# Moving two steps of a block inversion ahead in the program order of a hybrid attention and DeltaNet layer, with fewer and wider transfers for its bias and queries

## The chip, the cores and the metric

One core of a Trainium2 chip runs the kernel. The metric is the device time in microseconds (us) of one execution. The kernel before took 1246.18 us in the median of three runs (1244.01 to 1246.87). One more execution was profiled; its rows are the ones that the text reads. Times inside the program are given in us from the start of the profiled span.

The engines have short names in the rows: PE multiplies matrices (PEld is its weight load), DVE, ACT and POOL work on elements, SP only issues transfers. A transfer can also be issued by ACT or POOL.

## The reference: what is computed

One layer of an encoder on 1024 tokens of width 1024, in float32. The input is normalised and projected once; the columns of the projection feed two mixers, and their outputs are concatenated, projected, added to the input, and followed by a feed-forward part:

```
xn = rmsnorm(h); proj = xn @ w_in
attn = windowed_gqa(q_a, k_a, v_a, bias, in_window, sink)   # 8 heads of 64, 2 key/value heads, window 128
gdn  = gdn_mixer(qkv_g, z_g, a_g, b_g, ...)                 # 4 heads of 128, forwards and backwards in time
h = h + concat[attn, gdn] @ w_out
h = h + square(relu(rmsnorm(h) @ w_ffn_in)) @ w_ffn_out
out = rmsnorm(h)
```

The attention works on blocks of 128 queries, each against the key block before it, its own and the next one, with a bias that depends only on the distance of key and query. The DeltaNet part works on chunks. For each chunk and head it needs the inverse of a unit triangular matrix:

```
a_mat = where(strict, beta * kk * decay, 0)
t_mat = triangular_solve(eye + a_mat, eye, lower=True)
```

and then runs over the chunks one after the other, carrying a state. The kernel takes chunks of 128 tokens, so that there are 8 chunks, 4 heads and 2 directions: 64 triangular matrices of 128 x 128.

## The kernel before, in words

A program order is written down by Python generators, and a scheduler then fills the queue of each engine. Each engine works its queue strictly in order. The function `weave` (L55) merges several generators: each yields a price for what it has just emitted, and the stream with the smallest sum of prices divided by its weight goes next. The scheduler takes the order of emission as a priority: in its own timeline it gives an engine the earliest emitted instruction that is ready, so that the queues differ from the order of emission where something is not ready. Buffers come from pools with a fixed number of slots for each tag (`pg` 24, `pt` 12, `dbl` 2, `sc`, `wr` 4, `wh` and `wl` 3; psA and psB are 4 banks of PSUM each), and an instruction that writes into a new buffer waits for the release of the old one in that slot.

**The projection stage** (L1304). One stream holds the projections of v, z and of the attention's keys, values and queries: 24-matmul blocks of 128 output columns against half of the tokens (L125 to L129, three matmuls for each product since every operand is split into a coarse and a fine part). `proj_attn` (L468) ends the stream: one pair of blocks for keys and values, then four blocks for each of the two key/value heads' queries. For each query block DVE scales the result (L500), ACT rounds it (L501), POOL makes the remainder (L502), and four transfers on SP put the two parts of the two heads into the DRAM buffer `qad` (L506), 64 partitions each.

The other stream makes the triangular matrices (`prep`, L630), inverts their 32 x 32 diagonal blocks on DVE (`eliminate`, L665), lays the inverted blocks out in both orientations (`diag_blocks`, L685, four tiles that take all `sc` slots), and then `invert` (L695) builds the inverses of the 128 x 128 matrices. `invert` has four steps, each for two chunks, both directions and all heads. A step loads the matrices (L712), takes two result tiles and clears them on POOL (L716), copies the diagonal blocks into them with eight copies of 32 partitions on ACT (L720), and then goes through four rounds of small matmuls (L726; L736 with L740; L759; L767), each followed by an eviction (L729 on ACT; L745 and L752 on DVE; L761 on ACT; L770 on DVE). ACT also copies blocks into a helper tile (L750). In the stage only steps 0 and 1 are emitted; the projections use 16 of the `pg` slots for the transposed input (8 for each half of the tokens), 5 for keys and values.

**The next stage** (L1306 to L1324) begins with `bias_table` (L527): four `pg` tiles, each loaded by four transfers of 32 partitions on SP out of the DRAM buffer `biasd`, which `bias_rows` (L513) wrote much earlier. Then one stream holds the attention (`attention`, L603), the output projection of the attention (`out_attn`), that of the DeltaNet (`out_all`) and the transposes of the next part; the other holds steps 2 and 3 of `invert`, the forward scan, and the backward scan (`scan`, L774). The attention has 16 steps (8 query blocks, 2 key/value heads). A step computes scores on PE (L550, L551), adds the bias and takes the maximum on DVE (L552), takes the exponential on ACT (L564), scales on DVE and POOL (L569), transposes on PE (L579), copies on ACT (L581) and multiplies with the values (L591). Its query tile is loaded two steps ahead by one transfer of 128 partitions that POOL issues (`query`, L597, L600). The first query of each key/value head is asked for inside `proj_attn` (L509). The result of a query block goes out on SP (L595). A scan step loads its chunk on SP (L786, L798, L800) into `sc`, `pg` and `pt` slots, and its products are all at L805.

After these come the feed-forward products, with PE occupied nearly all the time.

Of the kernel before, what the change touches and what calls it, by code (L numbers as in the profile page):

```python
# [16 lines left out]
P = 128  # L17
SEQ = 1024
# [59 lines left out]
class Block:  # L78
# [389 lines left out]
    def proj_attn(self):  # L468
# [27 lines left out]
        for kv in range(2):  # L496
            raws = self.load_w(self.w_cols(w, C_AQ + 256 * kv, 256))
            for i, half, ps in self.pair(raws):
# [4 lines left out]
                for part, t in enumerate((qh.bitcast(F32), q)):  # L503
                    o = 64 * (kv ^ part)
                    for g in range(2):
                        nc.sync.dma_start(out=self.qad[kv, 2 * i + g, o:o + 64, half * HALF:(half + 1) * HALF],  # L506
                                          in_=t[64 * g:64 * g + 64, :])
# [5 lines left out]
    def bias_rows(self):  # L513
# [11 lines left out]
        nc.sync.dma_start(out=self.biasd, in_=row.unsqueeze(1).to_broadcast([8, 32, 512]))  # L525

    def bias_table(self):  # L527
        self.bias = []
        for b in range(4):
            t = self.pg((P, 2, 3 * P))  # L530
            for m in range(4):
                src = bass.AP(tensor=self.biasd.tensor,
                              offset=self.biasd.offset + 2 * b * 32 * 512 + P - 1 - 32 * m,
                              ap=[[511, 32], [32 * 512, 2], [1, 3 * P]])
                self.nc.sync.dma_start(out=t[32 * m:32 * m + 32], in_=src)
            self.bias.append(t)
# [60 lines left out]
    def query(self, n, kv):  # L597

        q = self.pt((P, 4, P), F32R)
        self.nc.gpsimd.dma_start(out=q, in_=self.qad[kv, :, :, n * P:(n + 1) * P].rearrange("g c t -> c g t").bitcast(F32R))  # L600
        return q
# [93 lines left out]
    def invert(self, tt, steps):  # L695
# [10 lines left out]
        for i in steps:  # L706
# [11 lines left out]
            for d in range(2):  # L718
                for q in range(4):
                    nc.scalar.copy(out=t[d][blk(q), :, blk(q)], in_=ctt[d][blk(q), :, ns].rearrange("p x n -> p n x"))  # L720
# [8 lines left out]
            nc.scalar.copy(out=x32, in_=px)  # L729
            yield 1.4  # L730
            pyt, py = self.ps("psB", (P, 8, 32)), self.ps("psB", (P, 8, 32))
# [22 lines left out]
            yield 2.4  # L754
            px = self.ps("psB", (P, 8, 64))
# [493 lines left out]
    def build(self):  # L1249
        tc, nc = self.tc, self.nc  # L1250
        with (
# [8 lines left out]
            self.biasd = d("biasd", (8, 32, 512))[:]  # L1260
# [3 lines left out]
            self.qad = d("qad", (2, 4, P, SEQ))[:]  # L1264
# [5 lines left out]
    def phases(self):  # L1270
# [11 lines left out]
        for half in range(2):  # L1282
# [5 lines left out]
            else:  # L1288
# [16 lines left out]
                  (chain(self.prep(), self.eliminate(), self.diag_blocks(), self.invert(tt, (0, 1))), 100.0)))  # L1305
# [5 lines left out]
        def output():  # L1311
# [4 lines left out]
            while len(self.summed) < 4:  # L1316
# [6 lines left out]
                  (chain(self.invert(tt, (2, 3)), self.scan(0, tt[0], w_attn), self.load_wout(0, (2,)),  # L1323
# [69 lines left out]
```

## Time and profile before

| what | value |
|---|---|
| median of three runs | 1246.18 us |
| time of the profiled execution | 1245.29 us |
| its span, first to last instruction | 1243.6 us |
| mean granted TensorE clock | 0.983 |
| busy share of PE, DVE, ACT, POOL | 95%, 69%, 50%, 46% |
| moved by DMA | 187.62 MB, 151 GB/s over the span |
| SP's DMA queue, share of 16 engines | 37.2% |
| POOL's DMA queue, share of 16 engines | 2.0% |

A row of a table by stretches gives the stretch from start to end and its length, then for PE, PEld, DVE, ACT and POOL the busy time and the count, then the granted PE clock (1.00 is full), the busy share of the DMA engines and GB/s. A row of the timeline gives start, length, engine (SPq is SP's queue), line, operation, what is written and read, the count, and in brackets how long the engine had been idle and what ended that. A row of the waits says which engine waited at which line for whom: total, times, longest. A row of groups gives busy time and the mean of one in ns. PE's busy time counts modelled ends of matmuls, so 95% is not 95% of its peak.

### The profile page before, as it was taken

Reading aid. Unit: us, or ns where it says so; the run is one execution under the profiler, and the core shown is the slowest. Engines: PE = TensorE matmul, PEld = TensorE weight load, DVE = VectorE, ACT = ScalarE, POOL = GpSimd, SP = SyncE. Lnnn points to the kernel's source line nnn. Section 1 sums busy time; section 2 is a strip of 40 time slices with the busy share of each in tenths; the row PEclk is TensorE's granted clock in tenths of the full one; section 3 lists DMA queues with packets and bytes.
Section 4 is the critical chain, followed back from the end, with each engine's and each line's share of the span. In section 5 each row is a group of like instructions: output and inputs, shape, how many; then the busy total and the mean of one; then the engine's idle time right before and its main releaser. Section 6 shows DMA issues by size and latency. Waiting matters only on the chain. (4 is left out here: it accounts for less than half of the span.)

```text
span 1243.6 us, 18468 instructions
## 1 busy us (share of the span) xinstructions
PE 1179.3 (95%) x6482; PEld 962.8 (77%) x6482; DVE 854.0 (69%) x1466; ACT 620.9 (50%) x1347; POOL 574.4 (46%) x486
## 2 busy tenths in 40 slices
PE   6999999899879999997899999999999999999997
PEld 5788877778657778876788888888777888888885
DVE  4677667973378996677654453544579797887976
ACT  6455688354575752125464544545555433444343
POOL 5354312224422334234474535445365655665595
PEclk9999999899889999998999999999999999999999
DMA  6134344524746667222234444344679624434323
GB/s 240 52 117 141 104 167 140 180 81 135 172 145 172 168 220 263 96 83 84 86 120 154 151 153 144 144 158 147 214 263 320 235 84 155 152 133 138 98 89 136
DMA packets 121629, 187.62 MB, mean 151 GB/s; under 512 B 11043, under 2 KB 64416, under 8 KB 121537
## 3 DMA queue, kind: packets, MB, share of 16 engines
q1 hardware_dynamic: 96708, 152.58, 37.2%
q10 hardware_dynamic: 16381, 29.67, 6.2%
q0 software_dynamic: 8448, 4.20, 2.0%
q8 instruction: 51, 0.84, 0.3%
q14 instruction: 41, 0.34, 0.1%
HBM read 122.39 MB, written 63.49 MB: 149 GB/s over the span
## 5 line engine op out<-in xcount | busy, mean ns | idle before, releaser
L127 PE MATMUL psA<-pg,wh 128*128 128x512 f32 x416 | 164.8, 397 | 1.7 <-ACT pt L464 1.7
L129 PE MATMUL psA<-pg,wl 128*128 128x512 f32 x416 | 164.1, 395 | 0.0
L128 PE MATMUL psA<-pg,wh 128*128 128x512 f32 x416 | 163.7, 394 | 0.0
L123 POOL TENSOR_TENSOR wl<-wr,wh 128x512 fp32r<-128x512 f32 x44 | 66.7, 1536 | 159.6 <-ACT wh L122 129.4
L1168 DVE TENSOR_TENSOR pg<-pg 128x512 fp32r<-128x512 f32 x112 | 123.0, 1133 | 17.6 <-ACT pg L1167 17.6
L123 POOL TENSOR_TENSOR wh<-wr,wh 128x512 fp32r<-128x512 f32 x32 | 47.4, 1502 | 129.0 <-ACT wh L122 129.0
L128 PE MATMUL psA<-pg,pg 128*128 128x512 f32 x256 | 99.9, 392 | 0.4 <-POOL pg L123 0.3
L127 PE MATMUL psA<-pg,pg 128*128 128x512 f32 x256 | 99.3, 392 | 0.9 <-DVE pg L1213 0.9
L1085 ACT ACTIVATE pt<-pt 128x512 f32<-128x512 f32 x64 | 40.3, 632 | 119.3 <-DVE pt L1075 119.3
L129 PE MATMUL psA<-pg,pg 128*128 128x512 f32 x256 | 99.7, 390 | 0.0
L123 POOL TENSOR_TENSOR pg<-wr,pg 128x512 fp32r<-128x512 f32 x48 | 73.4, 1560 | 51.5 <-ACT pg L122 51.5
L127 PEld LDWEIGHTS psA<-pg,wh 128*128 128x128 f32 x416 | 78.6, 189 | 19.0 <-ACT pt L464 2.1
L128 PEld LDWEIGHTS psA<-pg,wh 128*128 128x128 f32 x416 | 78.6, 189 | 17.8 <-issue 0.9
L129 PEld LDWEIGHTS psA<-pg,wl 128*128 128x128 f32 x416 | 78.6, 189 | 16.8
L1167 ACT CAST pg<-pg 128x512 fp32r<-128x512 f32 x112 | 67.1, 620 | 40.4 <-DMA pg<-sd 29.3
L128 PE MATMUL psB<-pg,pg 128*128 128x512 f32 x192 | 74.9, 390 | 0.8 <-POOL pg L123 0.7
L129 PE MATMUL psB<-pg,pg 128*128 128x512 f32 x192 | 74.8, 390 | 0.2 <-DVE pg L1168 0.2
L127 PE MATMUL psB<-pg,pg 128*128 128x512 f32 x192 | 74.7, 389 | 0.0
L122 ACT CAST wh<-wr 128x512 fp32r<-128x512 f32 x76 | 43.6, 623 | 50.0 <-PE psA L128 30.0
L1075 DVE TENSOR_TENSOR pt<-psB,pt 128x512 f32<-128x512 f32 x39 | 26.9, 689 | 54.0 <-PE psB L129 29.5
L1075 DVE TENSOR_TENSOR pt<-psA,pt 128x512 f32<-128x512 f32 x39 | 26.8, 689 | 51.8 <-PE psA L129 36.3
L127 PEld LDWEIGHTS psA<-pg,pg 128*128 128x128 f32 x256 | 48.1, 188 | 12.6 <-DVE pg L1213 2.1
(395 smaller groups left out, 3265.3 us busy)
## 6 DMA issues: line engine op xcount, KB each, us to landing
sd<-pt ACTq DMA_DIRECT2D x112, 256.0 KB, 2.1
pg<-sd SPq DMA_DIRECT2D x112, 256.0 KB, 2.9
wr<-in_w_ffn_in SPq DMA_DIRECT2D x32, 512.0 KB, 3.6
wr<-in_w_in SPq DMA_DIRECT2D x22, 512.0 KB, 5.0
pg<-in_x SPq DMA_DIRECT2D x16, 512.0 KB, 6.7
wr<-in_w_ffn_out SPq DMA_DIRECT2D x16, 512.0 KB, 4.7
sc<-kvd SPq DMA_DIRECT2D x14, 512.0 KB, 6.0
kvd<-pt SPq DMA_DIRECT2D x16, 256.0 KB, 2.4
```

The source lines that it names most:

```text
L122: nc.scalar.copy(out=h, in_=raw)
L123: (eng or nc.gpsimd).tensor_tensor(out=l, in0=raw, in1=h.bitcast(F32), op=ALU.subtract)
L127: nc.tensor.matmul(ps, wh, xh, start=first, stop=False, skip_group_check=onto)
L128: nc.tensor.matmul(ps, wh, xl, start=False, stop=False, skip_group_check=onto)
L129: nc.tensor.matmul(ps, wl, xh, start=False, stop=last, skip_group_check=onto)
L1075: self.nc.vector.tensor_tensor(out=out, in0=in0, in1=in1, op=ALU.add)
L1085: self.nc.scalar.activation(out=c, in_=c, func=AF.Relu)
L1167: nc.scalar.copy(out=s[:, 0], in_=raw)
L1168: v.tensor_tensor(out=s[:, 1], in0=raw, in1=s[:, 0].bitcast(F32), op=ALU.subtract)
```

## The change

All four steps of `invert` are emitted in the projection stage, and none in the next. Inside a step, the copies of the diagonal blocks are no longer made at its beginning: those of the second direction go to DVE and are emitted behind the first round of matmuls, those of the first direction stay on ACT, are emitted behind the second round, and are tied behind the eviction L729 on ACT (`issue_after` adds that order and nothing else). The query parts are written to `qad` in another layout with one transfer of 128 partitions for each part instead of two of 64. A query tile is read by two transfers of 64 partitions on SP instead of one of 128 partitions on POOL. `biasd` holds each row 128 times instead of 32, so that each bias tile is read by one transfer of 128 partitions instead of four of 32.

```
-                    o = 64 * (kv ^ part)
-                    for g in range(2):
-                        nc.sync.dma_start(out=self.qad[kv, 2 * i + g, o:o + 64, half * HALF:(half + 1) * HALF],
-                                          in_=t[64 * g:64 * g + 64, :])
+                    nc.sync.dma_start(out=self.qad[kv, part, i, :, half * HALF:(half + 1) * HALF], in_=t)
...
-        nc.sync.dma_start(out=self.biasd, in_=row.unsqueeze(1).to_broadcast([8, 32, 512]))
+        nc.sync.dma_start(out=self.biasd, in_=row.unsqueeze(1).to_broadcast([8, P, 512]))
...
-            for m in range(4):
-                src = bass.AP(tensor=self.biasd.tensor,
-                              offset=self.biasd.offset + 2 * b * 32 * 512 + P - 1 - 32 * m,
-                              ap=[[511, 32], [32 * 512, 2], [1, 3 * P]])
-                self.nc.sync.dma_start(out=t[32 * m:32 * m + 32], in_=src)
+            src = bass.AP(tensor=self.biasd.tensor, offset=self.biasd.offset + 2 * b * P * 512 + P - 1,
+                          ap=[[511, P], [P * 512, 2], [1, 3 * P]])
+            self.nc.sync.dma_start(out=t, in_=src)
...
         q = self.pt((P, 4, P), F32R)
-        self.nc.gpsimd.dma_start(out=q, in_=self.qad[kv, :, :, n * P:(n + 1) * P].rearrange("g c t -> c g t").bitcast(F32R))
+        for part in range(2):
+            o = 64 * (kv ^ part)
+            src = self.qad[kv, part, :, :, n * P:(n + 1) * P].rearrange("i (g c) t -> c (i g) t", c=64)
+            self.nc.sync.dma_start(out=q[o:o + 64].bitcast(F32), in_=src)
...
             t = [flat(tt[d][i]) for d in range(2)]
-            for d in range(2):
+
+            def diagonal(d):
                 for q in range(4):
-                    nc.scalar.copy(out=t[d][blk(q), :, blk(q)], in_=ctt[d][blk(q), :, ns].rearrange("p x n -> p n x"))
+                    out, src = t[d][blk(q), :, blk(q)], ctt[d][blk(q), :, ns].rearrange("p x n -> p n x")
+                    nc.vector.tensor_copy(out=out, in_=src) if d else nc.scalar.copy(out=out, in_=src)
+
...
-            nc.scalar.copy(out=x32, in_=px)
+            moved = nc.scalar.copy(out=x32, in_=px)
             yield 1.4
+            diagonal(1)
...
             yield 2.4
+            with self.tc.issue_after(moved.ins):
+                diagonal(0)
...
-                  (chain(self.prep(), self.eliminate(), self.diag_blocks(), self.invert(tt, (0, 1))), 100.0)))
+                  (chain(self.prep(), self.eliminate(), self.diag_blocks(), self.invert(tt, range(4))), 100.0)))
...
-                  (chain(self.invert(tt, (2, 3)), self.scan(0, tt[0], w_attn), self.load_wout(0, (2,)),
+                  (chain(self.scan(0, tt[0], w_attn), self.load_wout(0, (2,)),
```

More of the change, by code (lines that the diff above doesn't have):

```diff
@@ L1259, in build @@
             d = lambda name, shape: dram.tile(list(shape), F32, name=name)
-            self.biasd = d("biasd", (8, 32, 512))[:]
+            self.biasd = d("biasd", (8, P, 512))[:]
             self.hd, self.sd = d("hd", (NT, P, D))[:], d("sd", (DFF // 256, 7, P, HALF))[:]
@@ L1263, in build @@
             self.zd, self.mad = d("zd", (GH, P, SEQ))[:], d("mad", (NT, P, HALF))[:]
-            self.qad = d("qad", (2, 4, P, SEQ))[:]
+            self.qad = d("qad", (2, 2, 2, P, SEQ))[:]
             self.ktd, self.qtd = d("ktd", (GH, P, SEQ))[:], d("qtd", (GH, P, SEQ))[:]
```

## The prediction

> **What bounds the kernel now.** I read the page first, for the busy shares:
>
> ```profile
> span 1243.6 us, 18468 instructions
> PE 1179.3 (95%) x6482; PEld 962.8 (77%) x6482; DVE 854.0 (69%) x1466; ACT 620.9 (50%) x1347; POOL 574.4 (46%) x486
> ```
>
> PE is the bound, and what a change can win is PE's idle time and PE's time at a lowered clock. So the second view is the table by stretches, cut where the stages meet (the columns are PE, PEld, DVE, ACT, POOL, clock, DMA):
>
> ```profile
> 260.00:299.00 39.00, 36.43 (x567) 29.33 (x566) 19.38 (x33) 26.61 (x44) 15.26 (x16) 1.00 0.34 107
> 299.00:326.00 27.00, 27.00 (x121) 22.33 (x120) 4.74 (x7) 6.82 (x11) 11.48 (x10) 1.00 0.68 180
> 326.00:369.00 43.00, 31.64 (x545) 24.25 (x543) 28.65 (x101) 32.50 (x81) 17.34 (x21) 0.80 0.57 143
> 369.00:461.00 92.00, 86.73 (x625) 70.12 (x622) 84.85 (x278) 58.48 (x168) 29.41 (x26) 1.00 0.65 188
> ...
> 526.00:535.00 9.00, 5.23 (x36) 4.09 (x34) 9.00 (x19) 2.21 (x7) 5.60 (x4) 1.00 0.35 117
> ...
> 332.00:343.00 11.00, 7.27 (x144) 5.93 (x143) 6.72 (x28) 8.23 (x24) 5.46 (x8) 0.66 0.60 142
> ```
>
> The projections end at 326; in their last 27 us PE has no gap, while DVE works 4.74 us and ACT 6.82 us. The hole is the next stretch, 326 to 369, in which the attention starts beside steps 2 and 3 of the inversion and the scan has not begun: PE idles 43.00 - 31.64 = 11.4 us, and at a mean clock of 0.80 its 31.64 busy us would be 25.3 at full clock, an estimated 6.3 us more. Together 17.7 us. From 369 to 461, attention and forward scan together, PE idles 5.3 of 92 us and DVE 7.2: both are nearly full. Which waits make the hole is told by PE's waits from 290 to 380:
>
> ```profile
> PE psB L767 <- ACT pt L761: 4.1, 3, 3.3
> PE psA L550 <- DMA pt<-qad: 2.8, 1, 2.8
> PE psA L550 <- DVE nm L552: 1.5, 1, 1.5
> PE psB L759 <- DVE pt L752: 1.4, 2, 0.8
> PE psB L805 <- DVE sc L823: 1.2, 1, 1.2
> PE psA L591 <- ACT pt L581: 1.1, 1, 1.1
> ```
>
> The longest wait at L767 (3.3) and those at L759 (1.4) belong to the inversion, 2.8 to a query that came late, 1.5 to scores that DVE had not taken off. The timelines of SP, POOL, DVE and ACT say why:
>
> ```profile
> 297.63 19.59 SPq L506 DMA_DIRECT2D qad<-pt  x20
> ...
> 332.63 0.58 SPq L535 DMA_DIRECT2D pg<-biasd  x1
> ...
> 360.17 1.24 SPq L798 DMA_DIRECT2D sc<-kvd  x1
> ...
> 306.58 1.00 POOL L600 DMA_DIRECT2D pt<-qad  x1 [5.62 <-DMA qad<-pt]
> ...
> 326.29 0.79 POOL L600 DMA_DIRECT2D pt<-qad  x1 [6.96 <-DMA qad<-pt]
> ...
> 336.93 0.42 DVE L552 CUSTOM_DVE_ANT_0 wr<-psA,pg 128x256 f32<-128x256 f32 x1 [3.96 <-DMA qad<-pt]
> ...
> 342.49 5.20 ACT L720 COPY pg<-sc 32x256 f32<-32x256 f32 x8
> ```
>
> SP's queue is full of small transfers for 20 us before the projections end, and the last bias transfer leaves only at 332.63. DVE's third score of the second attention step waits until 336.93; the row names `qad`, but that instruction reads a bias tile loaded last, so I read it as the bias. POOL stands still for 5.62 and 6.96 us because a query transfer heads its queue and `qad` isn't written yet; the query remainders (L502) behind it are what `qad` waits for. ACT spends 5.20 us in one piece on the inversion's diagonal copies, ahead of the attention's exponentials. And the scan's first load leaves at 360.17, since it needs `sc` slots that the inversion's blocks hold to the end of step 3.
>
> **The change part by part. Steps 2 and 3 move ahead of 326.** Their PE work costs what steps 0 and 1 cost among the projections, in the groups from 262 to 299 (two steps each; L736 runs side by side with L740):
>
> ```profile
> L759 PE MATMUL psB<-pt,dbl 64*64 64x64 f32 x64 | 2.9, 222 | 1.2 <-POOL pg L490 0.9 <-DVE pt L752 0.3
> ...
> L740 PE MATMUL psB<-pt,sc 32*32 32x32 f32 x64 | 2.5, 224 | 0.0
> ...
> L767 PE MATMUL psB<-pg,pt 64*64 64x64 f32 x48 | 2.3, 221 | 0.7 <-ACT pt L761 0.7
> ...
> L726 PE MATMUL psB<-sc,dbl 32*32 32x32 f32 x128 | 2.2, 227 | 0.0
> ```
>
> That is 2.9 + 2.5 + 2.3 + 2.2 = 9.9 us. PE has no gap there, so the projections end 9.9 us later, plus new stalls: between 0 (their rounds fit between blocks) and the 2.6 us that PE idled from 260 to 299 beside steps 0 and 1. I take 1.3, the middle, for the new order brings L729 ahead of the diagonal copies but the result tiles come late: by my count of slots 16 + 5 + 3 of the 24 `pg` are taken, so three of the four tiles for steps 2 and 3 wait until the first half of the transposed input is released, two blocks (48 matmuls at 27.00 / 121, 11 us) before the projections end. The first rounds (L726, L736, L759) write no result tile and need not wait; copies, L745 and L767 go into those 11 us. Queued on POOL behind the clears are L502 and weight splits; on DVE behind L745 the evictions L500, for which PE has psA banks in reserve.
>
> **The stretch after it** keeps its PE work without the inversion: 25.3 - 9.9 = 15.4 us at full clock. Gone are the waits 3.3, 1.4, 2.8 and 1.5, 9.0 of 11.4; 2.4 stay. What idle and slow clock the start of the attention then has lies between 0.9 us (15.4 at the rate of 369 to 461, 5.3 of 92) and 2.4 + 6.3 = 8.7 (the waits that stay, and all of the clock's loss). I take 5, near the middle: the scan fills PE from its first loads on, but a few us of attention alone remain. The row of 332 to 343 has the clock at 0.66 after single gaps of 2.8 and 1.5 us, so short gaps cost clock too. By the Trainium skill (TensorE: Matmul & The Clock Gate, HAM oscillation) only idle gaps over about 3.4 us lower the clock; by that the start would cost at most 2.4 and the sum would win 2.6 more. The trace disagrees with it, and decides.
>
> Sum: what stood at 369.0 stands at 326 + 9.9 + 1.3 + 15.4 + 5 = 357.6, 11.4 us earlier.
>
> **The transfers and copies.**
>
> ```profile
> L506 SPq DMA_DIRECT2D qad<-pt x32: 445/554/600, 297.6 to 333.8; - x32
> ...
> L600 POOL DMA_DIRECT2D pt<-qad x16: 740/788/1001, 306.6 to 423.0; - x16
> ...
> L535 SPq DMA_DIRECT2D pg<-biasd x16: 371/426/1352, 317.3 to 332.6; - x16
> ...
> L525 SPq DMA_DIRECT2D biasd<-pt x1: 808/808/808, 140.0 to 140.0; - x1
> ...
> L745 DVE TENSOR_SCALAR pg<-psB x12: 404/417/431, 275.1 to 363.2; 32x256 f32<-32x256 f32 x12
> ...
> L720 ACT COPY pg<-sc x24: 612/645/681, 263.7 to 347.1; 32x256 f32<-32x256 f32 x24
> ...
> pt<-qad POOLq DMA_DIRECT2D x16, 256.0 KB, 4.5
> pt<-pd SPq DMA_DIRECT2D x16, 256.0 KB, 6.7
> ```
>
> Writing `qad`: 16 issues of 0.554 go (8.9 us of SP ahead of 334). Bias: 12 issues of 0.426 go (5.1 us). These 14 us are what brings the first queries and the bias before the projections' end; their worth is in the 9.0 above, not added again. The fourfold write of `biasd` leaves at 140.0 and is first read at 317.3: 177 us cover it; at the 6.7 us in which 256 KB land below, its 2 MB would take 54, so nothing is charged, and the cover holds. Queries: 16 x 0.788 = 12.6 us leave POOL, and 32 issues come to SP, at the 0.43 to 0.55 of its neighbours 14 to 18 us over the 120 us of the attention, hidden while SP only waits; on SP's queue a load landed in 6.7 us (`pd`), on POOL's in 4.5 (`qad`). The Trainium skill says why that may be (DMA: Bandwidth & Descriptors, Queues, rings and completion order): what SP issues is consumed in ring order behind SP's own earlier loads, while an engine alternates between queues. It speaks against this move, by some 2.2 us on each query. With a lead of two attention steps I charge 0; without that cover it is the third rival. The 16 DVE copies cost between 0.417 (L745, the same shape) and 0.645 (the same copy on ACT), 6.7 to 10.3 us, of which half lies beside steps 0 and 1 and half beside 2 and 3, where DVE has 20 and 22 us free; 0, and uncovered at most 10.3 less what ACT gives up.
>
> **Later stages.** With the scan earlier against the other stream, the stretch 526 to 535, where DVE is full and PE idles 3.8 us, may close; against that the backward scan moves into the stretch where DVE is full already. Bounds +4 and -3, I take 0.
>
> In all: 1245.29 - 11.4 = 1233.9 for the profiled execution. The median of the runs is 0.9 above that execution, so 1234.8, rounded 1235. Own range of this case: best 9.9 + 0 + 15.4 + 0.9 gives 352.2 (16.8 won) and 4 more, 1225; worst 9.9 + 2.6 + 15.4 + 8.7 gives 362.6 (6.4 won) less 3, 1243.
>
> **The rivals.** *The inversion ends late.* If the clears and copies for the three late tiles don't fit into the 11 us, L767 and its waits (3.3, 1.4) stay behind the projections with half of the clock's loss (3): 11.4 - 7.7 = 3.7 won, 1242.5. For it: slots are the tightest thing here. Against: ACT and DVE are nearly empty then.
>
> *The attention can't fill PE alone.* Then the inversion was filler, and the hole reopens apart from the transfers' 2.8 and 1.5: 17.7 - 4.3 = 13.4 in place of 5, 8.4 less, 3.0 won, and with the late stages' -3 nothing: 1246. For it: ACT was busy 32.50 of 43 us, more than half with attention. Against: the scan is there at once, and from 369 on the two fill PE.
>
> *SP's queue becomes the wait, slower.* The queries now stand in one queue with the scan's loads, which wait for slots, and with the attention's stores. Waits of SP from 369 to 461, and the scores' group there:
>
> ```profile
> SPq L798 <- DVE sc L833: 7.5, 1, 7.5
> ...
> SPq L786 <- DVE wl L873: 4.0, 1, 4.0
> SPq L786 <- DMA pg<-in_w_out: 3.9, 1, 3.9
> ...
> 369.00:461.00 92.00, 19.36 (x80) 1.00 0.65 188
> ```
>
> 80 rows, 8 to a step, are 10 steps, 9.2 us each. A query's lead is 18.4 us, less 6.7 to land 11.7. It decides once SP stands longer than 11.7 us before a query: 7.5 + 4.0 + 3.9 = 15.4 in a row would make a step 3.7 us late. At half of the 10 steps that is 18.5 us against 11.4: 7.1 slower, 1253. Against: these waits lie apart, and the scheduler places the query by its own timeline.
>
> **How the numbers follow.** A measurement of this kernel can tell about 0.2% (2.5 us) from no change. The forecast has 0.62, all faster but 0.01; the late inversion 0.13 (0.09 faster, 0.04 same); the unfilled attention 0.12 (0.05 faster, 0.07 same); the SP queue 0.13, slower. Faster 0.75, same 0.12, slower 0.13. The range 1226 to 1247 takes in the first three cases nearly whole and leaves out the slower one.
>
> **What would show it.** Right: L726 to L770 of all four steps before the projections' end, which comes near 337; no wait of L550 for `qad` or of L552 for a transfer; the first scan load before 345; clock near 1.00 in the 30 us after; PE idle there below 5. Wrong: PE gaps over 2.6 us in the last 60 us of the projections; L767 after the first scores; L550 waiting for `pt<-qad` in mid-attention (SP); or the same 12 us of PE idle with the attention's ACT and DVE rows as releasers.

## The result and the profile after

| kernel | median, us | lowest to highest | profiled execution | its span | mean clock |
|---|---|---|---|---|---|
| before | 1246.53 (4 runs) | 1244.01 to 1249.2 | 1245.29 | 1243.6 | 0.983 |
| after | 1275.36 (4 runs) | 1275.15 to 1277.79 | 1275.2 | 1273.2 | 0.976 |

The changed kernel takes 1.0236 times as long, 95% interval 1.021 to 1.0262. It is 28.8 us slower; 1235 was forecast, in a range of 1226 to 1247.

The top of the page after, for the busy shares:

```profile
span 1273.2 us, 18419 instructions
PE 1191.8 (94%) x6482; PEld 970.5 (76%) x6482; DVE 851.3 (67%) x1482; ACT 611.6 (48%) x1331; POOL 562.0 (44%) x470
```

PE executes the same 6482 matmuls, but is busy 12.5 us longer with them: that is clock, 0.976 in the mean in place of 0.983. The other 17.1 us of the longer span are idle time. The table by stretches of after tells in which stage. The first row is a stage that the prediction did not look at. Then follow the projections with the last steps of the inversion (to 351, where the scores begin), the start of the attention (18 us of it, then 43), its middle, and the rest up to the feed-forward part:

```profile
138.00:185.00 47.00, 36.50 (x193) 28.62 (x192) 24.47 (x43) 30.55 (x77) 8.54 (x10) 0.93 0.51 81
...
311.00:351.00 40.00, 39.62 (x594) 31.78 (x591) 18.66 (x34) 17.42 (x29) 17.43 (x18) 1.00 0.54 180
351.00:369.00 18.00, 13.85 (x86) 11.95 (x85) 13.36 (x58) 9.47 (x30) 3.21 (x3) 0.91 0.90 287
351.00:394.00 43.00, 37.81 (x251) 31.22 (x249) 38.13 (x143) 27.33 (x79) 10.85 (x9) 0.96 0.82 256
394.00:486.00 92.00, 83.01 (x556) 65.66 (x555) 79.05 (x277) 55.00 (x170) 23.94 (x18) 0.96 0.44 138
486.00:653.00 167.00, 144.18 (x724) 120.36 (x723) 94.85 (x193) 51.51 (x117) 62.04 (x58) 0.94 0.32 109
```

The first stretch in before:

```profile
138.00:185.00 47.00, 46.38 (x247) 36.94 (x246) 32.25 (x58) 40.07 (x101) 11.83 (x13) 1.00 0.49 146
```

Two things are to be seen. In the first row, 10.5 us of idle PE that were not there before. In the last, 22.8 us of idle and a clock of 0.94, at the end of the attention and behind it, where no edit was made. Between them the projections' end is nearly without a gap (0.4 us idle in 40), as in before, and the attention's start is no longer the great hole: in its first 43 us PE idles 5.2 us at a clock of 0.96, against 11.4 at 0.80. The whole stage, from the first scores to the first copy of a feed-forward product, still takes 302.1 us in after (350.9 to 653.0) and 300.3 in before (325.9 to 626.2), though in after no inversion is left in it. PE's waits from 311 to 653 name the releasers (in after, L545 is the scores, L809 the scan, L922 the transposes in `out_gdn`, the DeltaNet's output for one chunk, and L210 the transposes of normalised rows for the next part):

```profile
PE psA L922 <- DVE wr L919: 9.6, 3, 4.4
PE psB L809 <- DMA pt<-pd: 5.9, 2, 5.1
PE psB L210 <- DVE pg L206: 3.7, 1, 3.7
PE psA L545 <- DMA pt<-qad: 3.2, 1, 3.2
```

The inversion's waits of before (3.3 at L767, 1.4 at L759) are gone. In their place stand waits of the stage's end: 9.6 us for `out_gdn`'s scaled rows (4.9 in before), 5.9 for the scan's `pd`, 3.7 for a normalised row (2.3 in before).

**The first hole.** SP's timeline from 138 on, after and then before:

```profile
140.54 0.81 SPq L522 DMA_DIRECT2D biasd<-pt  x1
145.28 19.98 SPq L245 DMA_DIRECT2D wr<-in_w_in  x2
165.36 15.10 SPq L658 DMA_DIRECT2D atd<-pt  x2
```

```profile
140.00 0.81 SPq L525 DMA_DIRECT2D biasd<-pt  x1
144.75 5.57 SPq L245 DMA_DIRECT2D wr<-in_w_in  x2
150.41 0.99 SPq L660 DMA_DIRECT2D atd<-pt  x2
```

The issue of the bias write is no longer than before, 0.81 us. What it costs stands in the two rows below it: the next two issues on SP take 19.98 us in place of 5.57, and the two after them 15.10 in place of 0.99. The waits of after from 138 to 185 show who pays:

```profile
DVE pt L651 <- DMA biasd<-pt: 12.0, 1, 12.0
PE psB L642 <- DVE pt L651: 9.9, 1, 9.9
```

and DVE's timeline when the wait ends:

```profile
183.44 1.12 DVE L651 SCALAR_TENSOR_TENSOR pt<-pt,cc,psB 128x128 f32<-128x128 f32 x4 [12.04 <-DMA biasd<-pt]
```

DVE's products for the next chunk (L651) need a `pt` slot, and the releaser named is the bias write: it reads its rows out of a `pt` tile and holds that slot until it is done, 43 us after its issue. The stores to `atd`, which hold other `pt` slots, stand behind it on SP. PE then hangs on DVE.

### The profile page after: what moved, and what is told of

It is laid out like the page before. It is cut to its first block, busy times and chain, and to the rows that moved or that the text cites. A ratio compares the mean times of both kernels' runs of the same rounds, so it can differ in the third digit from the quotient of the medians.

```text
span 1273.2 us, 18419 instructions
## 1 busy us (share of the span) xinstructions
PE 1191.8 (94%) x6482; PEld 970.5 (76%) x6482; DVE 851.3 (67%) x1482; ACT 611.6 (48%) x1331; POOL 562.0 (44%) x470
## 4 chain that ended last, share of the span: by engine, by line
PE 68%; DVE 12%; DMA 8%; issue 5%; ACT 3%; POOL 3%; SPq 0%; POOLq 0%; ACTq 0%; DVEq 0%
PE psA L127 12%; PE psA L128 12%; PE psA L129 12%; PE psB L127 7%; PE psB L128 7%; PE psB L129 7%; PE psB L809 4%; DMA biasd<-pt 3%; PE psA L586 2%; DVE dbl L679 1%; DVE pt L677 1%; POOL pg L123 1%; DVE pt L1181 1%; PE psA L574 1%; ACT pg L656 1%
## 5 line engine op out<-in xcount | busy, mean ns | idle before, releaser
L127 PE MATMUL psA<-pg,wh 128*128 128x512 f32 x416 | 166.7, 401 | 2.2 <-ACT pt L464 2.1
L128 PE MATMUL psA<-pg,wh 128*128 128x512 f32 x416 | 165.5, 398 | 0.0
L122 ACT CAST wh<-wr 128x512 fp32r<-128x512 f32 x76 | 43.6, 622 | 50.2 <-PE psA L128 30.0
```

What stands on the lines that cost most here:

```text
L122: nc.scalar.copy(out=h, in_=raw)
L127: nc.tensor.matmul(ps, wh, xh, start=first, stop=False, skip_group_check=onto)
L128: nc.tensor.matmul(ps, wh, xl, start=False, stop=False, skip_group_check=onto)
```

## The experiments

The line numbers of the runs differ by a few lines; what a row shows is named each time. An expectation names its theories by letters of its own; the same letter in another round can mean something else.

**First round: which part is slow.** Four kernels. The first is the change with the bias image of before:

```
-        nc.sync.dma_start(out=self.biasd, in_=row.unsqueeze(1).to_broadcast([8, P, 512]))
+        nc.sync.dma_start(out=self.biasd, in_=row.unsqueeze(1).to_broadcast([8, 32, 512]))
```

(and the 16 loads of before.) The second is the kernel before with the wide image and its 4 loads alone. The third is the kernel before with the inversion's move alone:

```
-                  (chain(self.prep(), self.eliminate(), self.diag_blocks(), self.invert(tt, (0, 1))), 100.0)))
+                  (chain(self.prep(), self.eliminate(), self.diag_blocks(), self.invert(tt, range(4))), 100.0)))
...
-                  (chain(self.invert(tt, (2, 3)), self.scan(0, tt[0], w_attn), self.load_wout(0, (2,)),
+                  (chain(self.scan(0, tt[0], w_attn), self.load_wout(0, (2,)),
```

The fourth is the change with the same 2 MB image written from 128 partitions: the matmul that makes the 8 bias rows gets its 8 columns repeated 16 times, so that each row stands on 16 partitions, and each partition writes it 8 times.

```
-        nc.tensor.matmul(ps[:8, :], rb, oh, start=True, stop=True)
-        row = self.pt((8, 512))
-        nc.vector.tensor_copy(out=row, in_=ps[:8, :])
-        nc.sync.dma_start(out=self.biasd, in_=row.unsqueeze(1).to_broadcast([8, P, 512]))
+        nc.vector.tensor_copy(out=rb16, in_=rb.unsqueeze(2).to_broadcast([NBUCKETS + 1, 8, 16]))
+        nc.tensor.matmul(ps, rb16.rearrange("b h r -> b (h r)"), oh, start=True, stop=True)
+        row = self.pt((P, 512))
+        nc.vector.tensor_copy(out=row, in_=ps)
+        nc.sync.dma_start(out=self.biasd.rearrange("h (r s) x -> (h r) s x", r=16),
+                          in_=row.unsqueeze(1).to_broadcast([P, 8, 512]))
```

> The change with the bias image as it was (each row 32 times, 16 loads of 32 partitions). Theory A, the wide bias write holds SP's queue: in the changed kernel the two weight loads behind it took 20.0 us to issue (5.6 before), the matrices behind them 15.1, and PE waits 9.9 us at the mask matmul. Without it the projections start their last part 12.4 us earlier: 1275.4 - 12 = 1263, still 17 us above the kernel before. Theory B, the loss is all in the attention stage and the 12 us would be waited for there anyway: 1273 to 1277.

> The kernel before with nothing but the wide bias image (each row 128 times, one load of 128 partitions for each tile). Theory A: the write of 2 MB costs 12 us at about 145 to 190 us, the 12 saved issues on SP near 320 give back at most 5: 1246.5 + 7 to 12 = 1253 to 1259. Theory B: within 3 us of 1246.5.

> The kernel before with nothing but the order of emission changed: all four steps of the inversion beside the projections, copies, queries and bias as before. Theory C, the early inversion is itself the loss (the projections end 12 us later, and the scan, free to start early, takes PE and DVE from the attention and is missing as cover at the end of the stage): 1250 to 1262. Theory D, moving the inversion wins what was forecast and the transfers on SP spoil it: 1233 to 1243.

> The change whole, but the bias row is made on 128 partitions instead of 8 (the matmul's weights repeat each head 16 times), and each partition writes its row 8 times: the same 2 MB, the same image, another spread of the source. In the changed kernel the write went at 51 GB/s for some 40 us, as did the 0.5 MB before. If the rate comes from the 8 source partitions (theory A1) it goes near 200 GB/s and is done in 10 us: 1263 or up to 3 less, like the narrow image. If it is the 2 MB as such that hold the queue (theory A2): 1270 to 1276.

| kernel | median, us | ratio to before, 95% interval |
|---|---|---|
| change with the narrow bias image | 1262.26 | 1.0147, 1.012 to 1.0174 |
| before with the wide image alone | 1251.97 | 1.0067, 1.004 to 1.0095 |
| before with the early inversion alone | 1264.75 | 1.0156, 1.0123 to 1.0189 |
| change with the spread bias write | 1263.19 | 1.015, 1.0125 to 1.0175 |

The write is one cause, worth 12 to 13 us of the 28.8. In the kernel before, the wide image costs 7.1, which is the write less what the 4 loads gain; that is a little under the 1253 to 1259 of theory A. It isn't the bytes: spread over the partitions, the same 2 MB cost nothing that a measurement can tell from the narrow image. The DMA issues between 138 and 185 show it, after first, the spread version below (KB each, then us from issue to landing; for the first row of after the profile has no landing):

```profile
biasd<-pt SPq DMA_DIRECT2D x1, 2048.0 KB
wr<-in_w_in SPq DMA_DIRECT2D x2, 512.0 KB, 31.2
atd<-pt SPq DMA_DIRECT2D x3, 256.0 KB, 12.1
```

```profile
biasd<-pt SPq DMA_DIRECT2D x1, 2048.0 KB, 7.6
wr<-in_w_in SPq DMA_DIRECT2D x4, 512.0 KB, 4.3
atd<-pt SPq DMA_DIRECT2D x8, 256.0 KB, 2.0
```

From 8 partitions the write is done when DVE goes on, after 43 us, and weights issued behind it land after 31.2 us; from 128 it has landed in 7.6. The ten us from 145 to 155 show the rate of all transfers together, again after first:

```profile
145.00:155.00 10.00, 10.00 (x53) 8.19 (x52) 9.90 (x15) 9.16 (x24) 7.18 (x6) 1.00 0.45 51
```

```profile
145.00:155.00 10.00, 10.00 (x54) 8.38 (x53) 10.00 (x15) 9.14 (x25) 6.04 (x5) 1.00 0.71 241
```

The DMA engines are busy 0.45 of the time and move 51 GB/s, in place of 241. The Trainium skill (DMA: Bandwidth & Descriptors, Why a DMA increments its semaphore by 16 and not by 1) says that a transfer is split over the largest number of engines, 16 at most, that divides the size of the slowest dimension on both its sides. By that it is 8 for this write, which agrees with the 0.45, and 16 from 128 partitions. That accounts for at most a factor of two of the 4.7 between the two rows, whose busy shares differ by 1.6; where the rest comes from, no run here shows.

The other cause is the early inversion itself: alone, and with none of the transfers, it makes the kernel 20 us slower, more than theory C expected. The 11.4 us that the forecast won with it and the transfers had the wrong sign. Not all of these 20 us need be the same loss as in the change: in this run the first scores come at 343.1, 5.3 us later than in the spread version, and PE waits 8.4 us in one piece for a query.

**Second round: why the early inversion is slow.** All of it on the version with the spread write. The queries go back to POOL's queue; the scan is held back in the emission by 14.8 units of price, what steps 2 and 3 had taken there (7.4 each); or the scan's weight falls. The fourth kernel is the kernel before with all of the change's transfers, the bias write spread, and the inversion where it was.

```
-            self.nc.sync.dma_start(out=q[o:o + 64].bitcast(F32), in_=src)
+            self.nc.gpsimd.dma_start(out=q[o:o + 64], in_=src.bitcast(F32R))
```

```
-                  (chain(self.scan(0, tt[0], w_attn), self.load_wout(0, (2,)),
+                  (chain(iter([14.8]), self.scan(0, tt[0], w_attn), self.load_wout(0, (2,)),
```

```
-                         self.scan(1, tt[1], w_gdn)), 95.0)))
+                         self.scan(1, tt[1], w_gdn)), 86.0)))
```

> The version with the spread bias write (1263.2 us), and the queries issued by GpSimd again instead of SyncE, in the new layout. If queries that stand on SP's queue behind the scan's loads are what slows the attention (theory Q, the prediction's third rival), the 31 us by which the last attention value came later shrinks and the time falls by over 5 us, to 1250-1258. If the queue of the queries does not matter (theories S and F), 1261 to 1265.

> The version with the spread bias write (1263.2 us), and the scan held back in the emission by 14.8 units, what steps 2 and 3 of the inversion took there before, so that scan and attention stand against each other as in the kernel before. Theory S (the scan runs ahead of the attention, is over before out_all begins, and is then missing as cover): the hole at the start of the attention comes back in part, the gaps of L922 and L210 behind 550 us go, and the time falls to 1248-1256. Theory F (the inversion was filler for time in which PE idles anyway, wherever that lies; only its place among the projections, where PE has no gap, costs): the idle time moves back to the start and the total stays, 1260 to 1267.

> The version with the spread bias write (1263.2 us), and the scan's share in the emission cut from 95 to 86 against the output's 100, so that it starts at once but ends about 20 us later. Theory S: the scan fills the start and lasts to cover the first out_gdn chains, so the time falls most of all of these, to 1244-1253. Theory F: the PE work that can cover is the same, spread thinner; 1258 to 1266.

> The kernel before with the change's transfers alone: the 128-row bias image, written from 128 partitions, 4 bias loads, the new layout of the queries on SyncE; the inversion and the diagonal copies stay as they were. If the bias write costs little once it is spread and the queries' queue does not matter, the waits of 2.8 (query) and 1.5 us at the start of the attention go and it runs at 1238-1246. If either costs (theory Q, or a bias write that still fills SP's queue by its bytes), 1248-1255.

| kernel | median, us | ratio to before, 95% interval |
|---|---|---|
| spread, queries on POOL | 1264.42 | 1.0157, 1.014 to 1.0174 |
| spread, scan held 14.8 units | 1236.08 | 0.9928, 0.9913 to 0.9943 |
| spread, scan's weight 86 | 1246.18 | 1.0013, 0.9999 to 1.0026 |
| before with the transfers, spread | 1235.85 | 0.9931, 0.9913 to 0.9948 |

The queue of the queries does not matter. The place of the scan in the program order does: one number in front of it, which leaves PE, DVE, ACT and POOL the same number of instructions, is worth 27 us, more than was expected of it. The lower weight wins 17, but not as it was expected to: the scan does not end later (its last product starts at 534.3, against 539.2), the attention ends earlier (461.9, against 476.2), and the hold wins more. The transfers alone came out better than the 1238 to 1246 expected. Two rows each show where they lie, first without the hold, then with it; the stage is cut from the first scores to the first copy of a feed-forward product, and the lower rows count the scan's products alone (PE, PEld, clock, DMA share, GB/s):

```profile
338.00:642.40 304.40, 267.14 (x1523) 219.19 (x1522) 211.89 (x611) 133.89 (x364) 96.70 (x84) 0.93 0.43 138
```

```profile
338.00:369.00 31.00, 12.36 (x80) 11.29 (x80) 0.94 0.80 235
...
539.00:642.40 103.40, 0.46 (x5) 0.27 (x3) 0.89 0.22 74
```

```profile
337.90:616.20 278.30, 251.26 (x1525) 208.49 (x1525) 217.00 (x611) 133.82 (x364) 95.72 (x84) 0.99 0.47 153
```

```profile
338.00:369.00 31.00, 4.24 (x32) 4.05 (x32) 1.00 0.66 202
...
557.00:616.20 59.20, 0.65 (x6) 0.45 (x5) 0.94 0.22 76
```

Without the hold the scan takes 12.36 us of PE in the attention's first 31, with it 4.24. For that, the stage without the hold ends with 103 us in which there is almost no scan beside the output projections and their chains, with it 59. Idle time falls from 37.3 to 27.0 us, and the busy time by 15.9 at nearly the same number of matmuls, since the clock of the row is 0.99 in place of 0.93. PE's waits in the stage show the same, without the hold first:

```profile
PE psA L924 <- DVE wr L921: 9.6, 3, 4.3
PE psB L811 <- DMA pt<-pd: 7.0, 2, 6.2
PE psB L210 <- DVE pg L206: 3.7, 1, 3.7
```

```profile
PE psA L924 <- DVE wr L921: 5.9, 3, 4.1
...
PE psB L210 <- DVE pg L206: 2.3, 1, 2.3
```

The stage has two ends that must both be in. Behind the last product with the attention's values (L591 in before) come the attention's output projection and the rest of the stream; behind the last scan product (L805), the last `out_gdn` and what hangs on it. The starts of the last value product, the last scan product and the first feed-forward copy, from the rows of their lines, in us:

| kernel | last value | last scan | feed-forward copy | copy minus value | copy minus scan |
|---|---|---|---|---|---|
| before | 458.3 | 567.8 | 626.2 | 167.9 | 58.4 |
| after | 489.3 | 550.4 | 653.0 | 163.7 | 102.6 |
| early inversion alone | 485.6 | 546.9 | 644.9 | 159.3 | 98.0 |
| spread | 476.2 | 539.2 | 642.4 | 166.2 | 103.2 |
| spread, held 14.8 | 448.3 | 557.4 | 616.2 | 167.9 | 58.8 |
| before with the transfers, spread | 449.7 | 558.3 | 617.0 | 167.3 | 58.7 |

The rows behind the first and the fifth line:

```profile
L591 PE MATMUL psA<-pt,pg x88: 592/592/1112, 355.2 to 458.3; 128*64 128x512 f32 x88
```

```profile
L588 PE MATMUL psA<-pt,pg x88: 592/592/644, 352.5 to 448.3; 128*64 128x512 f32 x88
```

The remainder behind the last value is 159 to 168 us in all six, the one behind the last scan is 58 at the least. In before and in the two fast versions the copy comes at both distances at once: the streams end in balance. In the spread version, which does not have the first hole, the scan ends 28.6 us earlier than in before, where that is worth nothing, and the attention 17.9 later, which sets the end; in after the two are 17 earlier and 31 later. Behind the last value the time is the same with more scan to fill it or with less, first the spread version, then the held one:

```profile
476.20:642.40 166.20, 143.01 (x699) 120.01 (x696) 91.65 (x183) 49.89 (x113) 59.49 (x56) 0.91 0.30 104
```

```profile
448.30:616.20 167.90, 151.79 (x832) 128.60 (x829) 115.90 (x256) 57.61 (x141) 67.25 (x62) 0.98 0.36 125
```

Without the hold PE executes 133 matmuls fewer there, and idles 23.2 us in place of 16.1.

**Third round: how far that carries.** The change exactly as it is, with the hold and nothing else; the spread version with the 8 loads of x, behind which the scan's `pd` stood on SP, issued by POOL instead; a longer hold; and the hold with all diagonal copies on ACT.

```
+                  (chain(iter([14.8]), self.scan(0, tt[0], w_attn), self.load_wout(0, (2,)),
```

```
-            self.h[c] = self.load_x(c)
+            self.h[c] = self.pg((P, D))
+            self.nc.gpsimd.dma_start(out=self.h[c], in_=self.io["x"][0, c * P:(c + 1) * P, :])
```

```
-                  (chain(iter([14.8]), self.scan(0, tt[0], w_attn), self.load_wout(0, (2,)),
+                  (chain(iter([24.0]), self.scan(0, tt[0], w_attn), self.load_wout(0, (2,)),
```

```
-                    nc.vector.tensor_copy(out=out, in_=src) if d else nc.scalar.copy(out=out, in_=src)
+                    nc.scalar.copy(out=out, in_=src)
```

> The change exactly as it is, with the scan held back by 14.8 units and nothing else. If the slowdown is the sum of two causes that do not touch each other, the bias write (12 to 13 us) and the lost interlock of scan and attention (27 us), then 1275.4 - 27 = 1248 (1245 to 1252), and the 12 us stall at L651 is still there. If the hold only helps when the scan's loads come early, or the bias write's loss is won back by it, 1235 to 1243 or over 1256.

> The version with the spread bias write (1263.2 us), and the 8 loads of x for the attention's output issued by GpSimd, so that no load of the scan stands behind them on SyncE's queue. Theory S1 (the largest part of the loss is this place in SyncE's queue: 6.2 us of waiting for pd and the clock lowered after it): the gap near 482 us goes and the time falls to 1252-1256. Theory S2 (the loss is that the scan is over before out_all begins): the gap may go, the rest stays, 1257 to 1264.

> The version with the spread bias write and a hold of 14.8 (1236.1 us), with 24 units instead. If what counts is that scan matmuls are left to cover the out_gdn chains (theory S), more hold fills the gaps near 563 and 571 us but opens the attention's start further: 1232 to 1238. If 14.8 was a lucky order, 1240 to 1262.

> The version with the spread bias write and a hold of 14.8 (1236.1 us), with all diagonal copies on ACT again, at their new places. The prediction charged nothing for the 16 copies on DVE and gave them no gain either: 1234 to 1238. If ACT had become the wait of the early inversion without the split, 1238 to 1244 and a later end of L773.

| kernel | median, us | ratio to before, 95% interval |
|---|---|---|
| after, scan held 14.8 units | 1247.87 | 1.0024, 1.0012 to 1.0037 |
| spread, x loads on POOL | 1262.61 | 1.0134, 1.0111 to 1.0157 |
| spread, scan held 24 units | 1250.27 | 1.0038, 1.0015 to 1.0061 |
| spread, held 14.8, copies all on ACT | 1237.62 | 0.9941, 0.9922 to 0.996 |

The hold gives the change as it is 27.5 us back, and what stays is the bias write, with DVE's wait of 12.1 us at L651 still there: the two causes add up. The split of the diagonal copies makes no difference that these intervals tell. The wait for `pd` was no cause. With the x loads off SP it is down to 0.3 us, but the time is the same; PE's waits there from 460 to 560 have another one in its place:

```profile
PE psA L925 <- DVE wr L922: 6.2, 2, 4.3
PE psB L811 <- DVE sc L824: 4.0, 1, 4.0
```

And more hold is not better, against the expectation of theory S: at 24 units the scan ends at 570.7, the feed-forward copy comes at 632.7, 62.0 us behind it, while the attention is done at 449.9. Now it is the scan that is late.

**Fourth round: balance, or the start.** Open was whether the two ends have only to be in balance, or whether the attention's first steps must be free of the scan. No hold but a scan at weight 70; half of the hold; and a hold of 8 units in the kernel before with the transfers, which is in balance without one.

```
-                         self.scan(1, tt[1], w_gdn)), 95.0)))
+                         self.scan(1, tt[1], w_gdn)), 70.0)))
```

```
-                  (chain(iter([14.8]), self.scan(0, tt[0], w_attn), self.load_wout(0, (2,)),
+                  (chain(iter([8.0]), self.scan(0, tt[0], w_attn), self.load_wout(0, (2,)),
```

```
-                  (chain(self.invert(tt, (2, 3)), self.scan(0, tt[0], w_attn), self.load_wout(0, (2,)),
+                  (chain(self.invert(tt, (2, 3)), iter([8.0]), self.scan(0, tt[0], w_attn), self.load_wout(0, (2,)),
```

> The version with the spread bias write and no hold (1263.2 us), with the scan's share cut from 95 to 70 (86 gave 1246.2). Theory B (balance: the next stage begins at the later of the last attention value + 167 us and the last scan matmul + 58 us, and the best order is the one in which both are the same): the attention ends near 450 and the scan near 560, 1234 to 1243. Theory H (the attention's first steps must be free of the scan, which only the hold does): the attention stays late, 1245 or more.

> The version with the spread bias write, with a hold of 8 units, half of the 14.8. Theory B: the last attention value near 462, halfway between 476 and 448, the next stage 167 us behind it, and 1244 to 1256. Theory H: the first attention steps are free already, 1234 to 1240.

> The kernel before with the change's transfers (spread bias write, 1235.9 us), in balance without a hold (449.7 + 167 and 559.1 + 58), and a hold of 8 units put ahead of its scan. Theory B: the scan ends some 8 to 12 us later and sets the end, 1242 to 1250. If a later scan is good by itself, under 1234.

| kernel | median, us | ratio to before, 95% interval | last value, last scan, copy |
|---|---|---|---|
| spread, scan's weight 70 | 1259.53 | 1.0117, 1.0089 to 1.0146 | 464.4, 580.8, 642.6 |
| spread, scan held 8 units | 1245.2 | 0.9997, 0.9976 to 1.0018 | 462.0, 545.8, 627.7 |
| before with the transfers, held 8 | 1251.11 | 1.0057, 1.0035 to 1.0079 | 453.0, 573.4, 635.1 |

In all three the copy comes within 4 us of the later of value + 167 and scan + 58: 639 (by the scan), 629 (by the value) and 631 (by the scan), measured 642.6, 627.7 and 635.1. So the rule for the end holds, with the two constants of the second round. Read from the rows of all 19 kernels here it holds within 4 us, but for the early inversion alone, where the copy comes 7.7 us earlier. It tells which end is late, not why a stream ends when it does. Half a hold lands halfway as theory B has it, not theory H, and more hold on a version in balance is slower, by a little more than theory B expected. But theory B's forecast for the slow scan was wrong, and there theory H was right: at weight 70 the attention does not end at 450 but at 464.4, the scan late at 580.8. The scan's products took 9.62 us of PE in the attention's first 31, and then both streams stand still behind ACT; PE's waits in that stage:

```profile
PE psA L127 <- ACT pt L122: 7.0, 1, 7.0
PE psA L588 <- ACT pt L578: 6.9, 2, 6.0
```

Neither theory is enough alone: the end follows the later stream, but slowing the scan throughout made the scan late without letting the attention end early. Nor does the scan's work in the first 31 us settle where the attention ends: at weight 86 it took 11.78 us of PE there and the last value came at 461.9, with half a hold 7.48 and 462.0. What delays the attention in each order, and why ACT's copies (L578) and roundings (L122) come late at weight 70, stays open.

**Fifth round: what the transfers bring.** Each half of the transfers alone, in the kernel before: the queries (16 stores of 128 partitions, queries read on SP), and the bias (spread write, 4 loads).

```
-        self.nc.gpsimd.dma_start(out=q, in_=self.qad[kv, :, :, n * P:(n + 1) * P].rearrange("g c t -> c g t").bitcast(F32R))
+        for part in range(2):
+            o = 64 * (kv ^ part)
+            src = self.qad[kv, part, :, :, n * P:(n + 1) * P].rearrange("i (g c) t -> c (i g) t", c=64)
+            self.nc.sync.dma_start(out=q[o:o + 64].bitcast(F32), in_=src)
```

```
-            for m in range(4):
-                src = bass.AP(tensor=self.biasd.tensor,
...
-                self.nc.sync.dma_start(out=t[32 * m:32 * m + 32], in_=src)
+            src = bass.AP(tensor=self.biasd.tensor, offset=self.biasd.offset + 2 * b * P * 512 + P - 1,
+                          ap=[[511, P], [P * 512, 2], [1, 3 * P]])
+            self.nc.sync.dma_start(out=t, in_=src)
```

> The kernel before with the new layout of the queries alone: 16 stores in place of 32, queries read on SyncE. All transfers with the spread bias ran at 1235.9 against 1244.4 to 1246.5 for before. If the queries are what counts (8.9 us of SyncE's issues ahead of the bias loads, and the 2.8 us wait for qad), 1236 to 1240; if the bias is, 1243 to 1247.

> The kernel before with the 128-row bias image alone, written from 128 partitions and read in 4 loads instead of 16. From 8 partitions the same ran at 1252.0, 7.1 us slower than before. If the bias loads are what counts (5.1 us of SyncE's issues, the 1.5 us wait), 1236 to 1240; if the queries are, 1243 to 1247; if the 2 MB cost something even so, over 1247.

The queries alone run at 1237.68 us, ratio 0.9924 (0.9899 to 0.9949), the bias alone at 1240.93, ratio 0.9968 (0.9936 to 0.9999), against 1245.87 for before beside them. Either half gains by itself, 8.2 and 4.9 us, and both together gained 9.7, less than the sum. That would fit both clearing the same place, SP's queue ahead of the attention, but the intervals are too wide to show it. With the wide image from 8 partitions 7.1 slower than before and from 128 partitions 4.9 faster, the write from 8 costs 12.0 us in the kernel before too. PE's waits from 320 to 380 of the version with both have neither the 2.8 us for `qad` nor the 1.5 us for the scores' eviction:

```profile
PE psA L576 <- ACT pt L578: 3.3, 1, 3.3
PE psB L805 <- DVE sc L823: 1.2, 1, 1.2
PE psB L759 <- ACT pt L750: 1.2, 1, 1.2
```

So the 28.8 us come apart into four terms, all from medians above. The bias write from 8 partitions costs 1275.4 - 1263.2 = 12.2; the scan's place costs 1263.2 - 1236.1 = 27.1; the early inversion with the scan in its place costs 1236.1 - 1235.9 = 0.2; the transfers gain 9.7. Together 29.8, from medians of separate rounds. The terms hold in this order only: beside the early inversion without a hold the transfers gain next to nothing (1264.8 without them, 1263.2 with them, spread), so that the 27.1 contain their lost gain. Five versions run faster than both kernels. Four of them can't be told apart (ratios 0.9924 to 0.9941): the held one with or without the split of the copies, the transfers alone, and the queries alone, which is the smallest edit.

## Why the prediction was wrong, point by point

*The inversion's cost among the projections* was right. It put 9.9 + 1.3 = 11.2 us on it and the scores at 337.2; in the spread version, in which the bias write doesn't disturb, they begin at 337.8. All four steps end before the scores, so the rival in which the inversion ends late is out.

*"177 us cover it ... nothing is charged"* is the first step that failed, 12.2 us. The prediction asked when the written rows are read. It did not ask what stands behind the write on SP's queue, where the timeline of before has the weights and the stores of `atd`, nor who needs the slot that the write reads from. It also took a rate from a transfer of 128 partitions (256 KB in 6.7 us) for one that leaves from 8.

*"What stood at 369.0 stands at 357.6"* is the second, and the largest, 27.1 us. It shifted the rest of the stage as one block: the first copy of a feed-forward product, at 626.2 in before, should have come at 614.8, and in the spread version it came at 642.4. But two streams start at 326 and 369, and their places against each other changed: the scan's first product starts at 351.3 in after, right beside the first scores, and not 43 us behind them. With the hold it starts beside them too, at 338.4, but goes on slowly: 4.24 us of PE in the first 31, in place of 12.36. The hole at the start did shrink, as forecast: in the spread version PE is busy 25.02 of the first 30 us, at a clock of 0.94. The row:

```profile
338.00:368.00 30.00, 25.02 (x162) 21.08 (x161) 25.00 (x101) 17.64 (x54) 5.73 (x5) 0.94 0.80 235
```

That is 5.0 us of idle and, estimated from the row's clock, 1.5 us of slow clock, together 6.5 against the 5 that were charged for both, and inside the bounds of 0.9 and 8.7. But what filled the hole was the scan's work, which in before lay beside the output projections, and there, in waits of PE that end 150 to 263 us later (487.8 to 601.3), the gain went out again.

*"Later stages ... I take 0"*, with bounds of +4 and -3, was where that should have stood; the scan's place took 27.1. The stretch 526 to 535 was not the place to look: the row to read was the end of the stage, where the waits of `out_gdn` (L918, 4.9 us in before) lie uncovered as soon as the scan is over. Of the two ends only one can be late; the prediction worked out neither remainder, though the rows of before have both, 167.9 and 58.4.

*"The attention can't fill PE alone"* came nearest among the rivals but had another mechanism and 1246 for it. With the scan held back and the inversion early, the attention is nearly alone at its start: from 338 to 369 PE is busy 23.32 of 31 us, 4.24 of them with the scan. These 7.7 us of idle time do not keep the version from 1236.1.

*"SP's queue becomes the wait"* had the right sign and the wrong cause: with the queries on POOL the time is the same (1.0157 against 1.015). One query is late at the start, for 3.2 us on SP and 8.4 on POOL; behind it the two-step lead covers the 32 issues, as the prediction said.

*The transfers' worth*, which it saw in 14 us of SP's issues before the attention, is confirmed in kind. In the kernel before they gain 9.7 us, more than the waits of 2.8 and 1.5 that it credited to them. In the change itself the wait for a query did not go, as the prediction had it: 3.2 us at L545. *The DVE copies* cost nothing that the intervals tell, as it said.

## What to carry to other kernels

When work is moved out of a stage that two streams share, do not slide the rest forward as a block: work out what remains behind each stream's last instruction and which end is late, and put the freed time into that stream. Filler was worth more here where chains lay uncovered, 150 us and more behind the hole that it filled. And a transfer that nobody reads for 177 us can still have a price, paid by whatever is issued behind it.

## What the runs showed of the hardware

While a 2 MB write from 8 partitions ran, all transfers together moved 51 GB/s (145 to 155 us of after), and two loads issued behind it on the same queue landed after 31.2 us; from 128 partitions it landed in 7.6 us. Its own issue took 0.81 us, as that of the 512 KB write in before did, and 0.59 from 128 partitions: the price stood in the rows of the next issues.

Waits of 2.1 and 1.8 us cost no clock in the held version. PE's waits of the held version up to 405 are the first fence, and its stretch from 338 to 369 is the second, at a clock of 1.00:

```profile
PE psA L588 <- ACT pt L578: 2.4, 2, 1.8
PE psA L576 <- DVE wr L566: 2.1, 1, 2.1
```

```profile
338.00:369.00 31.00, 23.32 (x148) 17.49 (x147) 26.66 (x102) 21.70 (x66) 8.72 (x7) 1.00 0.66 202
```

The spread version, with one wait of 3.2 us near the same place (it ends at 343.0), has 0.94 from 338 to 368, and 0.50 from 344 to 346, right behind the wait. The Trainium skill (TensorE: Matmul & The Clock Gate, HAM oscillation) gives as a rule that PE should have no idle gaps over about 3.4 us. The held version agrees with it, and the 3.2 us of the spread one are just under. The row of 332 to 343 in before, on which the prediction set the rule aside, does not: the wait of 2.8 us ends just ahead of it, at 331.6, and from 332 to 334 the clock is 0.53.
